# Row sums, 1 / rms and dilated shares through DRAM, and values overwritten by outputs, in a two-layer hybrid block

## The chip, the cores and the metric

One NeuronCore of a Trainium2 chip runs the whole program. The metric is the device time of one execution in microseconds (us). TensorE (PE) multiplies; VectorE (DVE), ScalarE (ACT) and GpSimd (POOL) work on elements; SyncE (SP) issues DMAs. Each engine runs its instructions in program order, and an instruction that waits holds up all those behind it on its engine.

## The reference

512 tokens of width 1024, two layers. Each layer adds a mixer, a cross attention to a memory of 256 tokens, and a gated feed-forward part; each reads an RMS norm of x.

```python
def hybrid_mixer(h, ...):                    # h = rms_norm(x)
    r_q, r_k, r_v, r_g, g_q, g_k, g_v, g_a, g_b, g_z, d_q, d_k, d_v, gates = split(h @ w_in)
    q, k = rotate(r_q), rotate(r_k)                       # retention: 4 heads
    o = retention_chunked(q, k, r_v, log_gamma)           # chunks with a carried state
    o_ret = rms_norm(o, ret_norm_g) * silu(r_g)
    c_q, c_k, c_v = split(silu(causal_depthwise_conv([g_q, g_k, g_v])))
    g = -exp(a_log) * softplus(g_a + dt_bias)             # log decay
    # per chunk: gc = cumsum(g); decay = exp(gc_i - gc_j)
    # A = I + strict_lower((beta k) k^T * decay); solve A u = beta v, ...
    o = gated_delta_chunked(l2_norm(c_q), l2_norm(c_k), c_v, g, sigmoid(g_b))
    o_gdn = rms_norm(o, gdn_norm_g) * silu(g_z)
    for window, dilation in ((128, 1), (512, 4), (2048, 16)):
        o_g, lse_g = dilated_window_attention(rope(d_q), rope(d_k), d_v, ...)
    wts = softmax(lse over the three groups)              # the dilated shares
    o_dil = sum(wts * o_g)
    gate = sigmoid(gates)
    return sum(gate[i] * (o_i @ w_br_i) for i in (ret, gdn, dil)) @ w_out

for l in range(2):
    x = x + hybrid_mixer(rms_norm(x, ..), ..)
    x = x + memory_cross_attention(rms_norm(x, ..), rms_norm(mem, ..), ..)
    x = x + conv_gated_mlp(rms_norm(x, ..), ..)
return rms_norm(x, final_norm_g)
```

## The kernel before

Every large product is made of three matmuls (`mm3`, L213 to L215): weights and activations are split into a rounded half (`wh`, `xgh`) and a rest (`wl`, `xgl`). SP fetches a slab of weights (`w`, two buffers, L187), ACT rounds it to `wh` (L202), DVE subtracts to get `wl` (L203), three buffers each.

A scheduler orders the instructions of every engine by what it thinks will be ready; `first()` and `soon()` raise priorities. The mixer's main line goes from product to product (`rva`, `rg`, `g`, `rqk`, `dqk`, `dv`, gates), and short generators in a list `side` are stepped between its products, each up to its next `yield`: decays, inverse, attention and scan of the gated delta part, retention, heads. `finish()` drains the list.

- `rms` (L305): sums of squares by token through TensorE (`_ss`, L312), 1 / rms on DVE (`rc`), then a row of it over all partitions: one 128x128 matmul for each block of 128 tokens (`_rp`, L317) and a copy on ACT (L320). The mixer (`nm`) also wants it by strided tokens: four more `_ss` matmuls.
- `gdn_decays` (L424): running sums of the log decay by one matmul (`gps`), then their rows over all partitions by sixteen matmuls (`gr`, L464), from which ACT makes |difference| and exp.
- `gdn_inverse` (L484): blocks of A go through DRAM (`Ad`, `Ag`, `Td`; all issued on the queue `DQ`, which is SP's); 31 steps on DVE invert the 32x32 blocks (`fs` L517, `Tg` L519); four 32- and 64-wide rounds on TensorE (`y` L539, `x` L549) join them. `gk` (L498) is the last product that A needs.
- `gdn_scan` and `retention` carry states over the four token blocks; outputs `og` and `oret` have their own regions; retention is put into `side` after `finish()`, the heads after that.
- `dilated` (L748): shares by softmax over the groups, widened on POOL (`dw`) and turned into rows by 32 matmuls in two layers of 16 (`dr`, L839).

Of the kernel before, what the change touches and what calls it, by code (L numbers as in the profile page):

```python
# [9 lines left out]
F32 = mybir.dt.float32  # L10
# [8 lines left out]
P = 128  # L19
# [5 lines left out]
H = 4  # L25
# [76 lines left out]
def tile_hybrid(ctx, tc, xT, memT, pos, wts, cst, kst, prm, rows, outT):  # L102
    nc = tc.nc
    V, S, G, PE = nc.vector, nc.scalar, nc.gpsimd, nc.tensor
    DQ = nc.sync
# [252 lines left out]
    def load_x(src, pieces=((0, 4), (4, 8))):  # L358
        xt = [region(("r3", "r8")[i], [4, T], f"x{i}") for i in range(2)]
# [64 lines left out]
    def gdn_decays(l, ab, rb, res):  # L424
# [28 lines left out]
        V.tensor_scalar(gp, gps, -1.0, None, ALU.mult)  # L453
# [29 lines left out]
    def gdn_inverse(l, kT, ssv, res):  # L483
# [98 lines left out]
    def gdn_scan(l, kT, qT, vb, res):  # L582

        U, attn, ceg, eg, egl, ekl = (res[n] for n in ("A", "attn", "ceg", "eg", "egl", "ekl"))
        o = region("r2", [NB, H, P], f"og{l}")
        ssq = small("ssg", 16)
        res.update(og=o, ssg=ssq)
        S0 = None
        for b in range(NB):
            us = slice(b * H, (b + 1) * H)  # L590
            if b < NB - 1:
                kp = pg(f"kp{b}", (H, P))
                transposes(kp, lambda h: kT[:, h, blk(b)])
                ks = tg(f"ks{b}", (H, P))
                V.tensor_tensor(ks, kp, over(ekl[:, us], P), ALU.mult)
# [30 lines left out]
            yield 1  # L626
            if b:
                qS = pg(f"qS{b}", (H, P))
                for h in range(H):
                    PE.matmul(qS[:, h, :], lhsT=qT[:, h, blk(b)], rhs=S0[:, h, :], start=True, stop=True)  # L630
                V.tensor_tensor(o[:, b], qS, over(eg[:, us], P), ALU.mult)
            op = pg(f"op{b}", (H, P))
            for h in range(H):
                PE.matmul(op[:, h, :], lhsT=attn[:, b * H + h, :], rhs=vn[:, h, :], start=True, stop=True)
            if b:
                V.tensor_tensor(o[:, b], o[:, b], op, ALU.add)
            else:
                S.activation(o[:, b], op, AF.Copy)
            sq = tg(f"osq{b}", (H, P))
            for h in range(H):  # L640
                i = b * H + h
                S.activation(sq[:, h, :], o[:, b, h, :], AF.Square, accum_out=ssq[:, i:i + 1])
            if b < NB - 1:
# [11 lines left out]
    def retention(l, rqk, rv, dec, res):  # L655

        o = region("r7", [NB, H, P], f"oret{l}")
        ssq = small("ssr", 16)
        res.update(oret=o, ssr=ssq)
        ks, states = [], []  # L660
        for j in range(2):
            ks.append(tg(f"rk{j}", (NB - 1, P)))
            states.append(tg(f"rst{j}", (NB - 1, P)))
# [3 lines left out]
            V.tensor_tensor(ks[j].rearrange("p b (e d) -> p (b e) d", e=2),  # L667
                            tpz.rearrange("p b (e d) -> p (b e) d", e=2),
                            over(dec[:, K_KD + 6 * j:K_KD + 6 * j + 6], 64), ALU.mult)
        for j in range(2):  # L670
# [3 lines left out]
            sps = [pool(f"rs{h}", (NB, P)) for (h, r), pool in zip(pair, (pa, pg))]  # L674
# [20 lines left out]
            yield 1  # L695
            yield 1
            ips = [pool(f"ri{h}", (NB - 1, P)) for (h, r), pool in zip(pair, (pa, pg))]

            def before(b, e):
                r = pair[e][1]  # L700
                return PE.matmul(ips[e][:, b - 1, :], lhsT=rqk[r, j, blk(b)], rhs=states[j][r][:, b - 1],
# [3 lines left out]
            ops = [pool(f"ro{h}", (NB, P)) for (h, r), pool in zip(pair, (pa, pg))]  # L705
# [3 lines left out]
            for (h, r), ip, op in zip(pair, ips, ops):  # L709
                S.activation(o[:, :, h, :], op, AF.Copy)  # L710
# [37 lines left out]
    def dilated(l, dq, dk, dv0, dv12, kc):  # L748
# [64 lines left out]
        for i, o in enumerate((oA, oB)):  # L813
# [593 lines left out]
```

## Time and profile before

| | |
|---|---|
| three runs | 2114.33, 2116.84, 2120.52 us (median 2116.84) |
| profiled execution | 2120.04 us, span 2118.2 us, mean granted clock 0.993 |
| PE busy | 2070.4 us of the span, 98% |
| DVE, ACT, POOL busy | 64%, 44%, 20% |
| chain that ended last | PE 86%, DVE 9%, DMA 2% |
| DMA | 95 GB/s on average |

The time of an engine is read against the span, and within a stretch against the stretch's length; what is missing there is idle time. A matmul's own duration overlaps the next one, so its cost in a packed row is the distance from start to start.

### The profile page before, as it was taken

What the parts mean: (1) busy time and instruction counts of PE and PEld (TensorE: products, weight loads), DVE (VectorE), ACT (ScalarE), POOL (GpSimd) and SP (SyncE); (2) the same over time, 40 slices, a digit from 0 to 9 for tenths busy, and PEclk for the clock granted to TensorE, in tenths of its full rate; (3) what the DMA queues carried; (4) which work ended last, traced back from release to release, by engine and by line L of the source; (5) the groups of instructions that cost most, each with busy time, mean ns of one, the idle gap of its engine ahead of it and who ended that gap; (6) DMA issues with size and microseconds to landing.
All of it is one profiled execution on the core that took longest, in us unless ns stands there. A gap on an engine that the chain in (4) does not pass through costs nothing.

```text
span 2118.2 us, 28765 instructions
## 1 busy us (share of the span) xinstructions
PE 2070.4 (98%) x10697; PEld 1736.2 (82%) x10697; DVE 1359.2 (64%) x2479; ACT 926.9 (44%) x1897; POOL 423.4 (20%) x427
## 2 busy tenths in 40 slices
PE   7999999999999999999999999999999999999997
PEld 6787878788888888888888879787788888888886
DVE  6788566446577875476456964854565787745754
ACT  4654333443355543244344533344344464423433
POOL 7832101012130211011132220100222221100112
PEclk9999999999999999999999999999999999999998
DMA  4333212233332233333323242122323323332332
GB/s 146 100 106 104 75 51 95 71 115 110 99 110 86 94 100 95 95 100 100 111 90 99 80 109 70 48 88 95 117 90 90 119 81 100 100 95 95 100 95 85
DMA packets 69756, 201.52 MB, mean 95 GB/s; under 512 B 18352, under 2 KB 21296, under 8 KB 69104
## 3 DMA queue, kind: packets, MB, share of 16 engines
q1 hardware_dynamic: 67120, 192.28, 29.5%
q0 software_dynamic: 2352, 7.37, 1.2%
q8 instruction: 84, 1.38, 0.3%
q14 instruction: 56, 0.46, 0.1%
q10 hardware_dynamic: 144, 0.04, 0.0%
HBM read 192.78 MB, written 6.88 MB: 94 GB/s over the span
## 4 chain that ended last, share of the span: by engine, by line
PE 86%; DVE 9%; DMA 2%; issue 1%; ACT 1%; SPq 0%; DVEq 0%; ACTq 0%
PE gate L215 4%; PE gate L213 4%; PE gate L214 4%; PE uu L214 3%; PE ua L214 3%; PE uu L215 3%; PE ua L215 3%; PE uu L213 3%; PE ua L213 3%; PE dn L214 3%; PE dn L213 3%; PE dn L215 3%; PE dqk L213 2%; PE dqk L215 2%; PE dqk L214 2%; PE y L215 2%
## 5 line engine op out<-in xcount | busy, mean ns | idle before, releaser
L202 ACT ACTIVATE wh<-w 128x512 fp32r<-128x512 f32 (+2 forms) x689 | 428.8, 624 | 849.1 <-PE dn L214 128.7
L203 DVE TENSOR_TENSOR wl<-w,wh 128x512 fp32r<-128x512 f32 (+2 forms) x689 | 509.7, 742 | 346.1 <-ACT wh L202 326.4
L213 PE MATMUL gate<-xgh,wh 128*128 128x512 f32 x384 | 151.2, 394 | 0.9 <-ACT wh L202 0.9
L215 PE MATMUL gate<-xgh,wl 128*128 128x512 f32 x384 | 151.6, 395 | 0.0
L214 PE MATMUL gate<-xgl,wh 128*128 128x512 f32 x384 | 150.9, 393 | 0.0
L213 PE MATMUL ua<-xgh,wh 128*128 128x512 f32 x320 | 124.5, 389 | 0.0
L214 PE MATMUL ua<-xgl,wh 128*128 128x512 f32 x320 | 124.5, 389 | 0.0
L215 PE MATMUL ua<-xgh,wl 128*128 128x512 f32 x320 | 124.5, 389 | 0.0
L213 PE MATMUL uu<-xgh,wh 128*128 128x512 f32 x320 | 124.5, 389 | 0.0
L214 PE MATMUL uu<-xgl,wh 128*128 128x512 f32 x320 | 124.5, 389 | 0.0
L215 PE MATMUL uu<-xgh,wl 128*128 128x512 f32 x320 | 124.5, 389 | 0.0
L213 PE MATMUL dn<-ah,wh 128*128 128x512 f32 x308 | 119.8, 389 | 0.0
L214 PE MATMUL dn<-al,wh 128*128 128x512 f32 x308 | 119.8, 389 | 0.0
L1146 POOL TENSOR_TENSOR fya<-fya,fyu 128x512 f32<-128x512 f32 x44 | 72.9, 1657 | 222.9 <-DVE fyu L1130 221.1
L215 PE MATMUL dn<-ah,wl 128*128 128x512 f32 x308 | 116.1, 389 | 0.0
L303 POOL TENSOR_TENSOR acc<-acc,sq 128x512 f32<-128x512 f32 x41 | 60.6, 1479 | 243.5 <-ACT sq L302 242.4
L868 POOL TENSOR_TENSOR mg<-mg,g 128x512 f32<-128x512 f32 x32 | 46.3, 1448 | 245.0 <-DVE g L866 244.9
L377 POOL TENSOR_TENSOR rot<-rot,tab 128x512 f32<-128x512 f32 x32 | 49.5, 1550 | 227.5 <-DVE rot L376 163.4
L213 PEld LDWEIGHTS gate<-xgh,wh 128*128 128x128 f32 x384 | 72.2, 188 | 15.8 <-ACT wh L202 1.2
L215 PEld LDWEIGHTS gate<-xgh,wl 128*128 128x128 f32 x384 | 72.1, 188 | 15.5 <-issue 0.7
L214 PEld LDWEIGHTS gate<-xgl,wh 128*128 128x128 f32 x384 | 72.1, 188 | 15.5 <-issue 1.0
L213 PE MATMUL dqk<-xgh,wh 128*128 128x512 f32 x192 | 76.2, 397 | 2.6 <-DVE rot L376 1.1
(496 smaller groups left out, 5189.5 us busy)
## 6 DMA issues: line engine op xcount, KB each, us to landing
w<-in_wts SPq DMA_DIRECT2D x331, 512.0 KB, 3.6
tab<-tabs_d POOLq DMA_DIRECT2D x4, 512.0 KB, 4.4
x<-in_xT SPq DMA_DIRECT2D x2, 1024.0 KB, 6.1
mem<-in_memT POOLq DMA_DIRECT2D x8, 256.0 KB, 3.3
x_d<-x SPq DMA_DIRECT2D x8, 256.0 KB, 3.1
x<-x_d SPq DMA_DIRECT2D x2, 1024.0 KB, 6.6
out<-x SPq DMA_DIRECT2D x8, 256.0 KB, 2.3
w<-in_wts SPq DMA_DIRECT2D x7, 256.0 KB, 2.5
```

The source lines that it names most:

```text
L202: S.activation(wh[:, :m], w[:, o:o + m], AF.Copy)
L203: V.tensor_tensor(wl[:, :m], w[:, o:o + m], wh[:, :m], ALU.subtract)
L213: PE.matmul(out, lhsT=lh, rhs=rh, start=start, stop=False)
L214: PE.matmul(out, lhsT=lh, rhs=rl, start=False, stop=False)
L215: PE.matmul(out, lhsT=ll, rhs=rh, start=False, stop=stop)
L303: eng.tensor_tensor(acc, acc, sq, ALU.add)
L377: G.tensor_tensor(t, t, tab[:, 1, :], ALU.mult)
L868: G.tensor_tensor(mt, mt, g, ALU.add)
L1146: G.tensor_tensor(ya, ya, yu, ALU.mult)
```

## The change

Rows that TensorE made of short columns now go through DRAM: a DMA writes the column in the row's order, a second one reads it back to all partitions. That holds for `rms` (`_rd`, also for the strided order), for the running sums (`gd`, read straight into `attn`'s place, where ACT then works in place) and for the dilated shares (`sh`, `dr`). `DQ` becomes POOL's queue. `vb` stands in the place of `vT`, `og` in that of `vb`, `oret` in that of `rv`; regions are dealt anew. Retention and its head move from after `finish()` to the stage of the first `dqk` products, with PSUM tiles of one pool (`pa`) and smaller steps; `finish()` comes after the second `dqk` group; the tables of layer 0 are issued at once, no longer in `side`; in the scan and in the last round of the inverse steps are joined. The scan writes its output right after each state. Several buffers change their number.

```diff
-    DQ = nc.sync
+    DQ = nc.gpsimd
...
-        n = 2 * nb if perm else nb
-        rc, v = small("rc", 8, 3), small("rv", 8)[:, :n]
-        sp = pg(name + "_ss", (n,))
-        for b in range(n):
-            tok = blk(b) if b < nb else slice(b - nb, None, NB)
-            PE.matmul(sp[:, b:b + 1], lhsT=acc[:, tok], rhs=one, start=True, stop=True)
+        rc, v = small("rc", 8, 3), small("rv", 4)[:, :nb]
+        sp = pg(name + "_ss", (nb,))
+        for b in range(nb):
+            PE.matmul(sp[:, b:b + 1], lhsT=acc[:, blk(b)], rhs=one, start=True, stop=True)
         V.tensor_scalar(v, sp, 1.0 / D, EPS, ALU.mult, ALU.add)
-        rsqrt(rc[:, :n], v)
-        rps = pg(name + "_rp", (nb * P,))
-        for b in range(nb):
-            PE.matmul(rps[:, blk(b)], lhsT=rc[:, b:b + 1].to_broadcast([P, P]), rhs=ident,
-                      start=True, stop=True)
+        rsqrt(rc[:, :nb], v)
+
+        rd = dp.tile([nb * P], F32, name=name + "_rd")
         rr = tmp("row", [T], name + "_row", 1) if row is None else row
-        S.activation(rr, rps, AF.Copy)
+        with soon():
+            G.dma_start(rd.rearrange("(b p) -> p b", p=P), rc[:, :nb])
+            G.dma_start(rr, rd.partition_broadcast(P))
+        if perm:
+            G.dma_start(rc[:, nb:2 * nb], rd.rearrange("(p n) -> p n", n=NB))
         return rc, rr
...
+        gs = small("gs", 16)
+        V.tensor_copy(gs, gps)
+        V.tensor_scalar(gp, gs, -1.0, None, ALU.mult)
         S.activation(eg, gp, AF.Exp)
         A = region("r7", [16, P], f"A{l}")
         attn = region("r5", [16, P], f"attn{l}")
         res.update(A=A, attn=attn)
+        gd = dp.tile([16, P], F32, name=f"gd{l}")
+        with soon():
+            G.dma_start(gd.rearrange("u p -> p u"), gs)
+            G.dma_start(attn, gd.partition_broadcast(P))
+        yield 1
+        yield 1
+        S.activation(egl, attn[:, :, P - 1], AF.Exp, scale=-1.0)
         for b in range(NB):
-            yield 1
             us = slice(b * H, (b + 1) * H)
-            gr = pg(f"gr{b}", (H, P))
-            for h in range(H):
-                i = b * H + h
-                PE.matmul(gr[:, h, :], lhsT=gpos[:, i:i + 1].to_broadcast([P, P]), rhs=tri,
-                          start=True, stop=True)
-            S.activation(egl[:, us], gr[:, :, P - 1], AF.Exp, scale=-1.0)
-            for h in range(H):
-                i = b * H + h
-                S.activation(attn[:, i, :], gr[:, h, :], AF.Abs, bias=gp[:, i:i + 1])
+            for i in range(b * H, (b + 1) * H):
+                S.activation(attn[:, i, :], attn[:, i, :], AF.Abs, bias=gp[:, i:i + 1])
             S.activation(attn[:, us, :], attn[:, us, :], AF.Exp, scale=-1.0)
-            S.activation(ekl[:, us], attn[:, us, P - 1], AF.Copy)
             G.tensor_tensor(A[:, us, :], attn[:, us, :], again(low, H), ALU.mult)
+            yield 1
+        S.activation(ekl, attn[:, :, P - 1], AF.Copy)
+        for b in range(NB):
+            us = slice(b * H, (b + 1) * H)
             G.tensor_tensor(attn[:, us, :], attn[:, us, :], again(tri, H), ALU.mult)
...
-        o = region("r2", [NB, H, P], f"og{l}")
+        o = vb
...
-        o = region("r7", [NB, H, P], f"oret{l}")
+        o = rv.rearrange("p b (h d) -> p b h d", h=H)
...
-            sps = [pool(f"rs{h}", (NB, P)) for (h, r), pool in zip(pair, (pa, pg))]
+            sps = [pa(f"rs{h}", (NB, P)) for h, r in pair]
-            kvs = [pool(f"rS{h}", (NB - 1, P)) for (h, r), pool in zip(pair, (pa, pg))]
+            sts = []
+            for (h, r), sp in zip(pair, sps):
+                sts.append(ta(f"st{h}", (NB, P)))
+                V.tensor_tensor(sts[-1], sp, again(dec[:, h * P:(h + 1) * P], NB), ALU.mult)
+            yield 1
+            kvs = [pa(f"rS{h}", (NB - 1, P)) for h, r in pair]
             for (h, r), kv in zip(pair, kvs):
...
+            sh = dp.tile([NB * H, P], F32, name=f"sh{l}{i}")
+            G.dma_start(sh.rearrange("u p -> p u"), a)
             for hp in range(2):
-                wide = ta(f"dw{i}{hp}", (NB, 2, 64))
-                G.tensor_copy(wide, a.rearrange("p (n h o) -> p n h o", h=H, o=1)[:, :, 2 * hp:2 * hp + 2, :]
-                              .to_broadcast([P, NB, 2, 64]))
-                rows = pa(f"dr{i}{hp}", (NB, P))
-                for n in range(NB):
-                    PE.matmul(rows[:, n, :], lhsT=wide[:, n].rearrange("p h d -> p (h d)"), rhs=ident,
-                              start=True, stop=True)
+                rows = ta(f"dr{i}{hp}", (NB, P))
+                for e in range(2):
+                    G.dma_start(rows[halves[e]], sh.rearrange("(n h) p -> h n p", h=H)[2 * hp + e].partition_broadcast(64))
                 V.tensor_tensor(o[:, hp], o[:, hp], rows, ALU.mult)
...
+        if l == 0:
+            for _ in tables():
+                pass
         side.append(gdn_decays(l, ab, rb, res))
-        if l == 0:
-            side.append(tables())
...
-        vb = region("r4", [NB, H, P], f"vb{l}")
+        vb = vT.rearrange("p h (b t) -> p h b t", b=NB)
...
+        gh, gl = region("r5", [H, T], f"gh{l}", F32R), region("r6", [H, T], f"gl{l}", F32R)
+        rh, rl = region("r7", [H, T], f"rh{l}", F32R), region("r8", [H, T], f"rl{l}", F32R)
+
+        def retained():
+            yield from retention(l, rqk, rv, dec, res)
+            yield 1
+            yield from head_out(res["oret"], res["ssr"], rgz, rc, None, rh, rl, pa, "r")
+
+        side.append(retained())
         tab = load_tab(1, rr)
-        dqk = [region("r10", [4, T], f"dqk{l}0")]
+        dqk = [region(t, [4, T], f"dqk{l}{i}") for i, t in enumerate(("r10", "r4"))]
...
+        keys_and_queries(1)
         finish()
-        side.append(retention(l, rqk, rv, dec, res))
-        dqk.append(region("r1", [4, T], f"dqk{l}1"))
-        keys_and_queries(1)
-        gh, gl = region("r5", [H, T], f"gh{l}", F32R), region("r6", [H, T], f"gl{l}", F32R)
-        rh, rl = region("r3", [H, T], f"rh{l}", F32R), region("r8", [H, T], f"rl{l}", F32R)
-        dqk.append(region("r4", [4, T], f"dqk{l}2"))
-
-        def heads():
-            yield 1
-            yield from head_out(res["og"], res["ssg"], zgz, rc, rqs, gh, gl, pg, "g")
-            yield from head_out(res["oret"], res["ssr"], rgz, rc, None, rh, rl, pa, "r")
-
-        side.append(heads())
+        side.append(head_out(res["og"].rearrange("p h b d -> p b h d"), res["ssg"], zgz, rc, rqs, gh, gl, pg, "g"))
+        dqk.append(region("r1", [4, T], f"dqk{l}2"))
         keys_and_queries(2)
...
-        mg = [region(t, [4, T], f"mg{l}{i}") for i, t in enumerate(("r9", "r7"))]
+        mg = [region(t, [4, T], f"mg{l}{i}") for i, t in enumerate(("r9", "r3"))]
```

What this does to the order of instructions, at three places of layer 0. On SP before, around the DMAs behind the recursion (`Td` takes its result to DRAM, `T` and `A` are read from there; `w` are weights):

```order
L187 DMA w_28_2072<-in_wts 128x1024 [waits DMAHW7_49,DVE_49]
L522 DMA Td_1514<-Tg_1124 64x1024 [waits DVE_49]
L523 DMA Td_1514<-Ag_1123 64x1024 [waits DVE_49]
L532 DMA T_1517<-Td_1514 32x16x32 [waits DMAHW2_49]
L532 DMA T_1517<-Td_1514 32x16x32 x2
L529 DMA A_396<-Td_1514 32x16x32 [waits DMAHW3_49]
L529 DMA A_396<-Td_1514 32x16x32 [waits DMAHW0_49]
L529 DMA A_396<-Td_1514 32x16x32 [waits DMAHW1_49]
L529 DMA A_396<-Td_1514 32x16x32
L187 DMA w_29_2134<-in_wts 128x1024 [waits DVE_49]
```

On POOL after, the same DMAs (`tab` is a rotary table, `rot` a half of a rotation):

```order
L377 TENSOR_TENSOR rot<-rot,tab_1889 128x512 [waits DVE_49,Pool_49]
L387 DMA tab_2121<-tabs_d 128x1024 [waits DMASW2_49,DMASW3_49,DMASW1_49,Pool_49]
L527 DMA Td_1486<-Tg_1096 64x1024 [waits DVE_49]
L528 DMA Td_1486<-Ag_1095 64x1024 [waits DVE_49]
L537 DMA T_1489<-Td_1486 32x16x32 [waits DMASW4_49]
L537 DMA T_1489<-Td_1486 32x16x32
L537 DMA T_1489<-Td_1486 32x16x32 [waits DMASW0_49]
L534 DMA A_456<-Td_1486 32x16x32 [waits DMASW5_49]
L534 DMA A_456<-Td_1486 32x16x32
L534 DMA A_456<-Td_1486 32x16x32 [waits DMASW3_49]
L534 DMA A_456<-Td_1486 32x16x32
L377 TENSOR_TENSOR rot<-rot,tab_2121 128x512 [waits DVE_49] x3
```

The seven DMAs have left the weights' queue; on POOL they stand between the rotations of `rqk` and those of `dqk`.

On PE before, where the products `y` wait for `A`:

```order
L214 MATMUL rqk_2015<-xgl,wh_27_512_2022 128x512
L539 MATMUL y_1583<-A_396 32x32
L215 MATMUL rqk_2015<-xgh,wl_27_512_2023 128x512
L213 MATMUL rqk_2015<-xgh,wh_27_512_2022 128x512
L214 MATMUL rqk_2015<-xgl,wh_27_512_2022 128x512
L539 MATMUL y_1583<-A_396 32x32 x31
L215 MATMUL rqk_2015<-xgh,wl_27_512_2023 128x512
```

And after:

```order
L215 MATMUL dqk_2420<-xgh,wl_32_0_2424 128x512
L713 MATMUL ro_2300<-rv_160,st_2218 128x128 x4
L713 MATMUL ro_2301<-rv_160,st_2220 128x128 x2
L544 MATMUL y_1555<-A_456 32x32 x22
L720 MATMUL ri_2362<-rst_2158,rqk_1894 128x128
L544 MATMUL y_1555<-A_456 32x32 x9
L713 MATMUL ro_2301<-rv_160,st_2220 128x128 x2
L213 MATMUL dqk_2420<-xgh,wh_32_0_2423 128x512
L214 MATMUL dqk_2420<-xgl,wh_32_0_2423 128x512
```

Most of the `y` products have moved from the third unit of `rqk` into the fourth unit of the first `dqk` group (one of them stands in its third unit), and the retention's `ro` and `ri`, which came behind the whole scan before, stand around them.

On ACT before, around the first table load behind the running sums:

```order
L202 ACTIVATE wh_7_512_605<-w_7_599 128x512 [waits PE_49]
L471 ACTIVATE ekl<-attn_397 128x4 [waits Activation_49]
L469 ACTIVATE attn_397<-gr_490,gp 128x128
L352 ACT_TABLE_LOAD
L352 ACTIVATE sn_377<-ang_374 128x512 [waits Pool_49]
L401 ACT_TABLE_LOAD
L401 ACTIVATE gz<-rg_311,half 128x512 [waits PE_49]
L401 ACTIVATE gz<-rg_312,half 128x512 [waits PE_49]
L470 ACTIVATE attn_397<-attn_397 128x512 [waits Activation_49]
L401 ACTIVATE gz<-rg_313,half 128x512 [waits PE_49]
```

And after:

```order
L352 ACT_TABLE_LOAD
L352 ACTIVATE sn_309<-ang_306 128x512 [waits Pool_49]
L202 ACTIVATE wh_10_0_767<-w_10_765 128x512 [waits DMAHW2_49,PE_49,Activation_49]
L467 ACT_TABLE_LOAD
L467 ACTIVATE egl<-attn_457 128x16 [waits DMASW7_49]
L353 ACTIVATE ang_306<-ang_306 128x512 [waits Activation_49]
L412 ACTIVATE y_699<-cin_696,par 128x512 [waits DVE_49]
L413 ACTIVATE z_700<-cin_696,par 128x512
L471 ACTIVATE attn_457<-attn_457,gp 128x128 [waits Activation_49]
L471 ACTIVATE attn_457<-attn_457,gp 128x128 x9
L354 ACT_TABLE_LOAD
L354 ACTIVATE ang_306<-ang_306,c 128x512 [waits Activation_49]
```

Before, `attn` was made block by block as `gr` came from PE; now all of it waits for one DMA (the wait at `egl`), and two roundings of weights (`wh_10_512`, `wh_11_0`) stand behind it.

## Rows read from the trace of the kernel before

**Rows 1.** The first and fourth part of the page
```profile
PE 2070.4 (98%) x10697; PEld 1736.2 (82%) x10697; DVE 1359.2 (64%) x2479; ACT 926.9 (44%) x1897; POOL 423.4 (20%) x427
PE 86%; DVE 9%; DMA 2%; issue 1%; ACT 1%; SPq 0%; DVEq 0%; ACTq 0%
```

**Rows 2.** Stretches of the span: start:end, length, busy of each engine (instructions), clock, DMA
```profile
50.00:70.00 20.00, 17.31 (x86) 14.49 (x85) 8.58 (x11) 18.93 (x40) 17.22 (x16) 1.00 0.24 79
130.00:187.00 57.00, 55.93 (x274) 45.93 (x273) 55.83 (x119) 31.10 (x75) 13.25 (x17) 1.00 0.27 88
280.00:350.00 70.00, 64.60 (x359) 56.91 (x358) 56.92 (x139) 26.32 (x76) 11.10 (x9) 1.00 0.23 71
1310.00:1400.00 90.00, 85.77 (x464) 74.27 (x463) 67.12 (x161) 32.97 (x93) 10.52 (x8) 1.00 0.22 68
```

**Rows 3.** TensorE's groups by shape: records, busy, mean ns, idle before
```profile
L464 PE MATMUL gr<-c,gpos 128*128 128x128 f32 x64 | 8.6, 277 | 0.0
L839 PE MATMUL dr<-c,dw 128*128 128x128 f32 x64 | 8.4, 275 | 0.0
```

**Rows 4.** The chain that ended last, of several stretches: start, us, piece
```profile
41.33 0.91 PE rg L213 x4
...
619.57 0.79 PE nx_ss L312 x8
...
630.89 0.89 PE nx_rp L317 x8
...
1070.86 2.82 PE nm_ss L312 x16
```

**Rows 5.** The timeline of TensorE at four places: start, us, instruction
```profile
107.69 0.83 PE L498 MATMUL gk<-kT 128*128 128x128 f32 x6
...
193.19 0.22 PE L539 MATMUL y<-A 32*32 32x32 f32 x2 [1.02 <-DMA A<-Td]
...
1153.94 0.94 PE L498 MATMUL gk<-kT 128*128 128x128 f32 x7
...
1230.17 0.22 PE L539 MATMUL y<-A 32*32 32x32 f32 x2 [1.52 <-DMA A<-Td]
```

**Rows 6.** VectorE's groups by shape (first: 123.5 to 187 us; others: whole span)
```profile
L203 DVE TENSOR_TENSOR wl<-w,wh 128x512 fp32r<-128x512 f32 x20 | 15.3, 767 | 0.3 <-ACT wh L202 0.3
...
L375 DVE TENSOR_TENSOR rqk<-rqk,tab 128x512 f32<-128x512 f32 x8 | 5.5, 683 | 6.8 <-PE rqk L215 6.8
L376 DVE STREAM_SHUFFLE rot<-rqk 128x512 f32<-128x512 f32 x8 | 5.8, 726 | 0.0
```

**Rows 7.** The chain that ended last, 184 to 196 us
```profile
185.90 1.05 DVE Ag L520
186.96 3.11 DMA Td<-Ag
...
194.35 1.19 PE y L539 x62
```

**Rows 8.** The lines that issue DMAs from GpSimd: ns min/median/max, first and last start
```profile
L387 POOL DMA_DIRECT2D tab<-tabs_d x4: 577/586/597, 76.5 to 1251.0; - x4
...
L809 POOL DMA_DIRECT2D sd<-stA x2: 804/805/806, 405.4 to 1447.2; - x2
```

**Rows 9.** DMA issues: out<-in, count, KB each, median us from issue to landing
```profile
tab<-tabs_d POOLq DMA_DIRECT2D x4, 512.0 KB, 4.4
...
A<-Td SPq DMA_DIRECT2D x8, 64.0 KB, 2.9
...
sd<-stA POOLq DMA_DIRECT2D x2, 16.0 KB, 2.5
```

**Rows 10.** ScalarE's groups by shape, 40 to 75 us
```profile
L469 ACT ACTIVATE attn<-gr,gp 128x128 f32<-128x128 f32 x16 | 4.7, 380 | 0.0
...
L352 ACT ACT_TABLE_LOAD x1 | 1.3, 1283 | 0.0
```

**Rows 11.** Waits of TensorE: us in total, times, longest us
```profile
PE rva L213 <- ACT wh L202: 8.4, 1, 8.4
```

More of the change, by code (lines that the diff above doesn't have):

```diff
@@ L358, in load_x @@
     def load_x(src, pieces=((0, 4), (4, 8))):
-        xt = [region(("r3", "r8")[i], [4, T], f"x{i}") for i in range(2)]
+        xt = [region(("r7", "r8")[i], [4, T], f"x{i}") for i in range(2)]
         with first():
@@ L554, in gdn_inverse @@
         S.activation(Tm[32:64, :, 0:32], x32[32:64], AF.Copy, scale=-1.0)
-        for g in range(2):
-            yield 1
-            us = slice(8 * g, 8 * g + 8)
+        yield 1
+        halves = [slice(8 * g, 8 * g + 8) for g in range(2)]
+        yts = []
+        for g, us in enumerate(halves):
             y64 = pg(f"y64{g}", (8, 64))
@@ L584, in gdn_scan, with out @@
         U, attn, ceg, eg, egl, ekl = (res[n] for n in ("A", "attn", "ceg", "eg", "egl", "ekl"))
-        o = region("r2", [NB, H, P], f"og{l}")
+        o = vb
         ssq = small("ssg", 16)
         res.update(og=o, ssg=ssq)
-        S0 = None
+        S0, vn = None, None
+        def out(b, S0, vn):
+            us = slice(b * H, (b + 1) * H)
+            if b:
+                qS = pg(f"qS{b}", (H, P))
+                for h in range(H):
+                    PE.matmul(qS[:, h, :], lhsT=qT[:, h, blk(b)], rhs=S0[:, h, :], start=True, stop=True)
+                V.tensor_tensor(o[:, :, b], qS, over(eg[:, us], P), ALU.mult)
+            op = pg(f"op{b}", (H, P))
+            for h in range(H):
+                PE.matmul(op[:, h, :], lhsT=attn[:, b * H + h, :], rhs=vn[:, h, :], start=True, stop=True)
+            if b:
+                V.tensor_tensor(o[:, :, b], o[:, :, b], op, ALU.add)
+            else:
+                S.activation(o[:, :, b], op, AF.Copy)
+            sq = tg(f"osq{b}", (H, P))
+            for h in range(H):
+                i = b * H + h
+                S.activation(sq[:, h, :], o[:, h, b, :], AF.Square, accum_out=ssq[:, i:i + 1])
         for b in range(NB):
             us = slice(b * H, (b + 1) * H)
[L591 to L595, printed above, removed]
             if b == 0:
-                r = vb[:, 0]
+                r = vb[:, :, 0]
             else:
@@ L604, in gdn_scan @@
                     i = b * H + h
-                    V.scalar_tensor_tensor(r[:, h, :], kS[:, h, :], ceg[:, i:i + 1], vb[:, b, h, :],
+                    V.scalar_tensor_tensor(r[:, h, :], kS[:, h, :], ceg[:, i:i + 1], vb[:, h, b, :],
                                            ALU.mult, ALU.add)
+            if b < NB - 1:
+                kp = pg(f"kp{b}", (H, P))
+                transposes(kp, lambda h: kT[:, h, blk(b)])
+                ks = tg(f"ks{b}", (H, P))
+                V.tensor_tensor(ks, kp, over(ekl[:, us], P), ALU.mult)
             yield 1
@@ L625, in gdn_scan @@
                                                ALU.mult, ALU.add)
[L626 to L643, printed above, removed]
+                out(b, S0, vn)
                 S0 = S1
                 yield 1
+            else:
+                out(b, S0, vn)
     def together(calls):
@@ L695, in retention @@
             yield 1
[L696 to L701, printed above, removed]
-                                 start=True, stop=True)
-            together([lambda a=(b, e): before(*a) for b in range(1, NB) for e in range(2)])
-            ops = [pool(f"ro{h}", (NB, P)) for (h, r), pool in zip(pair, (pa, pg))]
+            ops = [pa(f"ro{h}", (NB, P)) for h, r in pair]
             for (h, r), st, op in zip(pair, sts, ops):
@@ L708, in retention, with before @@
                     PE.matmul(op[:, b, :], lhsT=st[:, b], rhs=rv[:, b, h * P:(h + 1) * P], start=True, stop=True)
-            for (h, r), ip, op in zip(pair, ips, ops):
                 S.activation(o[:, :, h, :], op, AF.Copy)
+            yield 1
+            ips = [pa(f"ri{h}", (NB - 1, P)) for h, r in pair]
+            def before(b, e):
+                r = pair[e][1]
+                return PE.matmul(ips[e][:, b - 1, :], lhsT=rqk[r, j, blk(b)], rhs=states[r][:, b - 1],
+                                 start=True, stop=True)
+            together([lambda a=(b, e): before(*a) for b in range(1, NB) for e in range(2)])
+            for (h, r), ip in zip(pair, ips):
                 for b in range(1, NB):
@@ L944, in values @@
             transposes(vp, lambda b: vT[:, h, blk(b)])
-            V.tensor_tensor(vb[:, :, h, :], vp, over(res["bk"][:, h::H], P), ALU.mult)
+            V.tensor_tensor(vb[:, h], vp, over(res["bk"][:, h::H], P), ALU.mult)
             done.append(h)
@@ L1222, in tile_hybrid @@
         rc, rr = rms(acc, NB, f"nx{l}")
-        oh, ol = region("r0", [H, T], f"xoh{l}", F32R), region("r7", [H, T], f"xol{l}", F32R)
+        oh, ol = region("r0", [H, T], f"xoh{l}", F32R), region("r3", [H, T], f"xol{l}", F32R)
         cross(l, (mgh, mgl), mrc, mrow, rr, oh, ol)
```

33 lines of the change are left out of this document (13 added, 20 removed).

## Prediction

> **What bounds the kernel now.** I read the page first: TensorE is busy 2070.4 of 2118.2 us, and the chain that ended last is 86% PE and 9% DVE [rows 1]. So there are two ways to win: take work from PE, or take away PE's idle time, which is 47.8 us in all. Then I asked for PE's idle time by stretches. It lies almost wholly in the two mixers. The reader should look at two kinds of stretch. From 130 to 187 us DVE is busy 55.8 of 57 us: there the chain runs through DVE, and PE, busy 55.9, only just keeps up. From 280 to 350 and from 1310 to 1400 us, where retention and the heads run, PE lacks 5.4 and 4.2 us [rows 2]. The rest of the kernel (cross attention, feed-forward) is packed, so PE work that goes there is a gain in full.
>
> A packed 128x512 matmul costs 0.91 / 4 = 0.228 us from start to start, a plain 128x128 one 0.89 / 4 = 0.22 (eight records are four matmuls), a transpose, one record, 0.11 [rows 4]. I take 0.114 for a 128x256 one, an estimate from half the columns.
>
> **PE work removed.** `gr` and `dr` are 64 records each [rows 3]: at 0.89 us for eight [rows 4], 7.1 us each. The four kinds of `_rp` are by the program 56 records: 6.2 us. The strided sums: `nm_ss` takes 2.82 us for sixteen records, `nx_ss`, which has no strided ones, 0.79 for eight [rows 4], so 2.0 us in each layer, 4.1. Together 24.5 us. The row copies on ACT and the `dw` copies on POOL go too; neither engine sets the end there, so they count nothing. Nothing is added on PE.
>
> **The recursion.** Before, the last `gk` ends at 108.5 us and the first `y` starts at 193.2, so 84.7 us pass; in layer 1 it is 1154.9 and 1230.2, so 75.3 [rows 5]. By the order, PE does there 254 (layer 1: 244) matmuls of 512 columns, 96 of 256, 32 (28) transposes and 16 products `ap`: 254 x 0.228 + 96 x 0.114 + 32 x 0.11 + 16 x 0.22 = 75.9 us, in layer 1 73.2. It loses 8.8 and 2.1 us, because `y` waits for the chain `Ag` copy, `Td`, `A` [rows 7] behind a saturated DVE.
>
> After, the `y` products stand later: 358 matmuls of 512, 29 of 256, 35 transposes and 30 products come first, 95.4 us; in layer 1 304, 96, 32 and 16, 87.3 us. But more DVE work stands before the recursion's end too. In layer 0: two more `wl` at 0.77, three more rotations of `rqk` at 0.68 + 0.73 + 0.68 [rows 6], the third step counted like L375, and some 1 us net of other evictions: 1.5 + 6.3 + 1.1 = 8.9 us. In layer 1 the same count gives 7.7.
>
> The DMAs behind it: before, the copy ends at 186.95 and the bulk of `y` starts at 194.35, 7.4 us [rows 7]. After, POOL issues one `Td` half behind the copy (0.6), waits for its landing (3.1), issues four `A` (4 x 0.6 = 2.4), and the last lands 2.9 us later: 9.0 us [rows 7 to 9]. I take 2 us more than before.
>
> So the chain needs 84.7 + 8.9 + 2 = 95.6 us for 95.4 us of PE work, and 75.3 + 7.7 + 2 = 85.0 for 87.3. The loss goes from 8.8 to about 1 and from 2.1 to about 1 (I leave 1 us each for waits on the way): a gain of 9. If the chain were late by 5 us more in each layer, the gain would be nothing. Behind the seven DMA issues on POOL stand the rotations of `dqk`: POOL is held for some 8.5 us, DVE's third rotation step waits for it, and `wl` behind that. DVE has about 10 us of its own work ahead of that step, so I cost it at nothing; without that cover it is up to 8.5 us per layer.
>
> **Retention and heads.** They bunch up behind the scan: DVE is busy 56.9 of 70 us, and PE lacks 5.4 and 4.2 us [rows 2]. Half of that work now runs beside the first `dqk` products. I let half of the idle time go: 4.8 us. The bounds are 0 and 9.6.
>
> **Rows through DRAM.** A write and a read take about 0.8 + 2.5 and 0.6 + 4.4 us [rows 8, 9], 8.3 us from the column to the row; before, PE and ACT needed about 2. For `nm`, `nk` and `nf` whole groups of products lie between and hide it. For `nx` the first eviction of the cross attention's queries waits; PE can go on into other PSUM tiles for most of it: 1 us lost per layer, 2 in all (bounds 0 and 10). No row shows a write of 2048 single values (`gd`, `sh`); the nearest are 0.59 us for a table of 128 long rows and 0.805 for 512 short pieces [rows 8]. By that slope it is 0.8 + 1536 x 0.00057 = 1.7 us, an estimate; the lower bound is 0.8. `sh` is read one branch later, hidden.
>
> **The decays in layer 0.** From 50 to 70 us ACT is busy 18.9 and POOL 17.2 of 20 us, and PE lacks 2.7 [rows 2]. ACT's sixteen |differences| at 0.38 and its table loads at 1.28 [rows 10] stay. After, all of them wait for one load of `attn`, which POOL issues behind three multiplications; I put its landing at about 62 us. Two roundings of weights stand behind it on ACT. I count 4.2 us of idle time for 2.7: 1.5 lost (bounds: 3 gained, 8 lost).
>
> **The sum.** -24.5 - 9 - 4.8 + 2 + 1.5 = -34.8 us on the profiled execution's 2120.04 (its span and about 2 us around it): 2085. That execution was 3.2 us above the median of 2116.84 and within the three runs; on the median it would be 2082. I say 2083.
>
> **A rule against the change.** The POOL queue is where the rows and a rule part. The table loads issued by POOL take 0.577 to 0.597 us each [rows 8], and they land 4.4 us later for 512 KB [rows 9]; nothing there looks starved. The Trainium skill, "SBUF — State Buffer", section "SBUF: two separate sides", says that GpSimd writes the descriptors of the DMAs it issues, and cannot while VectorE copies in a mode that holds their shared port; its example goes from about 620 to about 3100 ns. By that figure the 28 DMAs of the inverse would cost 28 x 2.5 = 69 us more; it is a reason for the first rival below, which is worked out without it.
>
> **Rivals.**
> - *POOL's queue becomes the bound; slower.* 28 DMAs of the inverse (14 in each layer: `Ad`, `Ag`, `Td`, `T`, `A`) now go one behind the other on POOL, on the one chain that has no slack. If each costs c instead of 0.6 us there, the end moves by 28 x (c - 0.6), and the gain of 34.8 is gone from c = 1.85 on. With c = 2.9, a whole landing [rows 9], it is +64 - 35 = +29: 2149, on the median 2146. For it: POOL waits in order, and rotations stand behind. Against it: the rows of the table loads.
> - *Only the removed work counts.* The waits move and stay as large: -24.5 + 3.5 = -21: 2099, on the median 2096. For it: an in-order machine with a saturated DVE finds a new place to wait. Against: PE has 14 to 20 us more work before `y`.
> - *The mixers' idle time goes altogether.* 47.8 us less the start, 8.4 [rows 11], and some 7 that I leave for the last norm and the output, an estimate, is 32; with 24.5 it is -57: 2063, on the median 2060. For it: each stage gets slack at once. Against: DVE stays saturated from 130 us on.
> - *The change does not do what it says:* the order shows the removed matmuls gone, so I give this none.
>
> **Chances.** Forecast 0.46, only the work 0.20, all idle time 0.13, POOL's queue 0.21. Runs of this kernel differ by 0.3% (2114.33 to 2120.52), so 0.3%, 6.4 us, is what can be told from no change. Forecast, work alone and idle time are all faster by more; within POOL's queue c near 1.85 gives no change. Faster 0.73, same 0.07, slower 0.20. The range goes from 2056, a little past the case without idle time, to 2126, where POOL's queue costs 2.1 us for each DMA; the forecast's own range is 2070 to 2095.
>
> **What would show it.** Right: no `gr`, `dr`, `_rp` on PE; `y` without a wait of more than 2 us; `Td` and `A` issued from POOL at about 0.6 us each; PE's idle time some 37 us in all instead of 47.8; cross attention and feed-forward of the old length but for the rows. Wrong: `y`, or `wl` behind a rotation, waits for POOL or its DMAs for over 5 us per layer; ACT sits at `egl` for over 5 us while PE waits for `wh`; or PE's first product behind each norm waits for a row.

## The result, and the profile after

The changed kernel takes 2195.09 us (median of four runs, 2193.12 to 2198.93) where the kernel before takes 2117.10: 1.037 of it, 95% interval 1.0349 to 1.0391. It is 78 us slower; 35 us faster was forecast.

The page of the changed kernel, engine line [rows 1]:

```profile
PE 2072.2 (94%) x10497; PEld 1731.0 (79%) x10497; DVE 1379.8 (63%) x2481; ACT 919.1 (42%) x1875; POOL 469.0 (21%) x489
```

The span of 2197.2 us is 79.0 longer. PE's idle time is 2197.2 - 2072.2 = 125.0 us where it was 47.8; that is 77.2 of the 79.0. Its busy time has not fallen, though the matmuls are gone. The reason shows in the waits of PE after (us in total, times, longest):

```profile
PE g L213 <- ACT wh L202: 15.1, 2, 10.6
PE ua L213 <- DVE cfa L1138: 11.9, 2, 6.4
PE nx_ss L310 <- POOL acc L303: 11.7, 2, 6.0
PE xq L215 <- DVE wl L203: 9.1, 2, 5.2
PE gate L215 <- DVE wl L203: 9.1, 2, 5.5
PE rva L213 <- ACT wh L202: 8.4, 2, 8.1
...
PE gate L213 <- ACT wh L202: 7.1, 3, 6.0
...
PE y L544 <- DMA A<-Td: 3.9, 2, 2.6
```

The wait of `rva` was there before [rows 11], `y` waited then too [rows 5], and `gate` waited 0.9 us for `wh`. The others are new, and are for ACT's `wh`, DVE's `wl` and `cfa`, POOL's `acc`: engines that are held up by something else. The DMA issues after (columns as in [rows 9]) name it:

```profile
tab<-tabs_d POOLq DMA_DIRECT2D x4, 512.0 KB, 4.1
...
nm_row<-nm_rd POOLq DMA_DIRECT2D x2, 256.0 KB, 4.5
...
A<-Td POOLq DMA_DIRECT2D x8, 64.0 KB, 4.3
...
sh<-k POOLq DMA_DIRECT2D x4, 8.0 KB, 11.3
...
nm_rd<-rc POOLq DMA_DIRECT2D x2, 2.0 KB, 9.3
...
gd<-gs POOLq DMA_DIRECT2D x2, 8.0 KB, 11.9
sd<-stA POOLq DMA_DIRECT2D x2, 16.0 KB, 2.5
...
nk_rd<-rc POOLq DMA_DIRECT2D x2, 1.0 KB, 9.7
nx_rd<-rc POOLq DMA_DIRECT2D x2, 2.0 KB, 9.0
nf_rd<-rc POOLq DMA_DIRECT2D x2, 2.0 KB, 9.4
```

All the writes of a column to DRAM (`_rd`, `gd`, `sh`), of 1 to 8 KB, take 9.0 to 11.9 us to land. The write of 16 KB that was there before, `sd`, still takes 2.5, and the table load 4.1. The norms' rows are read back in 4.2 to 4.5 us, as forecast; `attn`, 1 MB, takes 7.2. Two stretches of the changed kernel, and the first one's place in the kernel before (columns as in [rows 2]):

```profile
480.00:520.00 40.00, 27.66 (x103) 21.56 (x103) 18.16 (x28) 9.21 (x17) 10.88 (x12) 0.83 0.44 92
280.00:350.00 70.00, 70.00 (x373) 62.02 (x372) 53.24 (x115) 21.68 (x54) 12.72 (x9) 1.00 0.25 82
```

```profile
475.00:520.00 45.00, 45.00 (x228) 37.25 (x227) 29.62 (x57) 18.38 (x37) 13.84 (x14) 1.00 0.35 107
```

In the second, where PE lacked 5.4 us before, it lacks nothing. In the first, in the dilated stage, it lacks 12 of 40 us, where it lacked nothing before, and the granted clock is 0.83: a part of the stretch ran at 1.2 instead of 2.4 GHz, after PE's idle time. Right behind a wait of 6.00 us the gate products stand 0.43 us apart from start to start; from 493 us on it is 0.23 again. Over the whole span the granted clock is 0.971, before 0.993. That is why PE's busy time has not fallen.

What holds it, on POOL and then on DVE (start, us, instruction, idle before and its releaser):

```profile
476.95 1.18 POOL L848 DMA_DIRECT2D sh<-k  x1
...
489.19 2.48 POOL L852 DMA_DIRECT2D dr<-sh  x4 [9.97 <-DMA sh<-k]
```

```profile
488.38 0.18 DVE L838 TENSOR_TENSOR k<-k,stB 128x16 f32<-128x16 f32 x1 [10.62 <-DMA sh<-k]
```

POOL issues `sh` at 476.95 and stands 9.97 us until it has landed, because the reads `dr` are next in its order. DVE wants to write over the buffer that the DMA still reads, and stands 10.62 us. ACT, which takes DVE's result, stands as long; behind that, on ACT, stand the roundings of the weights (`wh`), and PE waits 6.0 us for them at its next gate product.

At the decays it is the row's own reader. In layer 1 ACT stands at `egl`, which reads `attn`, and PE waits for the rounded weights behind it; this is the longest single wait of the list:

```profile
1158.06 0.23 ACT L467 ACTIVATE egl<-attn 128x16 f32<-128x16 f32 x1 [12.87 <-DMA attn<-gd]
```

```profile
1161.76 0.80 PE L213 MATMUL g<-xgh,wh 128*128 128x512 f32 x1 [10.57 <-ACT wh L202]
```

At the norms it is POOL's order, and again a reader. POOL after, and PE behind it:

```profile
631.25 0.72 POOL L317 DMA_DIRECT2D nk_rd<-rc  x1 [1.58 <-DVE rc L289]
641.24 0.58 POOL L318 DMA_DIRECT2D macc<-nk_rd  x1 [9.27 <-DMA nk_rd<-rc]
641.85 1.27 POOL L303 TENSOR_TENSOR acc<-acc,sq 128x512 f32<-128x512 f32 x1
653.66 0.77 POOL L317 DMA_DIRECT2D nx_rd<-rc  x1 [10.55 <-DVE rc L289]
662.38 0.55 POOL L318 DMA_DIRECT2D nx_row<-nx_rd  x1 [7.96 <-DMA nx_rd<-rc]
```

```profile
643.17 1.87 PE L310 MATMUL nx_ss<-c,acc 128*128 128x1 f32 x8 [5.69 <-POOL acc L303]
```

The write of the memory's 1 / rms lands 9.3 us late for its own read; behind that read stands `acc`, the sum of squares of another norm, and PE waits 5.69 us for it. Then `nx_rd` takes its own 8 us. The row of the feed-forward's norm is late for its reader on DVE, `cfa`, for which PE waits 6.4 us at `ua`:

```profile
758.35 0.69 DVE L1138 TENSOR_TENSOR cfa<-up,nf_row 128x512 f32<-128x512 f32 x1 [9.85 <-DMA nf_row<-nf_rd]
```

There is one more way, on another queue. A weight fetch of SP that is issued while a column's write is on its way is late too. The fetch next behind `nf_rd` in the changed kernel (745 to 747 us), then in `row_write`, an experiment below that writes the same values in longer pieces (718 to 722 us):

```profile
w<-in_wts SPq DMA_DIRECT2D x1, 512.0 KB, 11.8
```

```profile
w<-in_wts SPq DMA_DIRECT2D x1, 512.0 KB, 4.5
```

The median of all fetches is 3.5 us in both. For the fetch behind `gd` ACT's `wh` waits:

```profile
64.95 0.63 ACT L202 ACTIVATE wh<-w 128x512 fp32r<-128x512 f32 x1 [7.04 <-DMA w<-in_wts]
```

How much of the 78 us comes by each of these ways is not shown.

### The profile page after: what moved, and what is told of

The parts are those of the page before. It is cut to its first block, busy times and chain, and to the rows that moved or that the text cites. A ratio compares the mean times of both kernels' runs of the same rounds, so it can differ in the third digit from the quotient of the medians.

```text
span 2197.2 us, 28429 instructions
## 1 busy us (share of the span) xinstructions
PE 2072.2 (94%) x10497; PEld 1731.0 (79%) x10497; DVE 1379.8 (63%) x2481; ACT 919.1 (42%) x1875; POOL 469.0 (21%) x489
## 5 line engine op out<-in xcount | busy, mean ns | idle before, releaser
L203 DVE TENSOR_TENSOR wl<-w,wh 128x512 fp32r<-128x512 f32 (+2 forms) x689 | 515.7, 751 | 344.3 <-ACT wh L202 318.8
L213 PE MATMUL ua<-xgh,wh 128*128 128x512 f32 x320 | 126.4, 395 | 11.9 <-DVE cfa L1138 11.9
L213 PE MATMUL g<-xgh,wh 128*128 128x512 f32 x192 | 77.4, 403 | 16.5 <-ACT wh L202 15.1
```

Source lines behind the costliest of these rows:

```text
L203: V.tensor_tensor(wl[:, :m], w[:, o:o + m], wh[:, :m], ALU.subtract)
L213: PE.matmul(out, lhsT=lh, rhs=rh, start=start, stop=False)
```

## The experiments

Theory A: the writes in pieces of 4 bytes land late, and the rows' readers, the order of POOL, and buffers that the DMA still reads pass the delay to all engines. Rival B: GpSimd's queue itself is the cost, above all for the inverse's DMAs. Rival C: the earlier retention and the shared places are. Rival D: GpSimd makes its descriptors slowly. Kernels of one group ran on one chip, each group on another; the first result's chip is not on record. The kernel before took 2120.25, 2120.29 and 2120.46 us in the three groups.

**Group 1: take one kind of row back to TensorE.** `rms_pe`:

```diff
-            G.dma_start(rd.rearrange("(b p) -> p b", p=P), rc[:, :nb])
-            G.dma_start(rr, rd.partition_broadcast(P))
+            PE.matmul(rps[:, blk(b)], lhsT=rc[:, b:b + 1].to_broadcast([P, P]), rhs=ident, ...)
+        S.activation(rr, rps, AF.Copy)
```

> The changed kernel with only the rows of 1 / rms made by TensorE again (_rp matmuls, strided _ss, copy on ACT). Theory A (the writes of single 4-byte values to DRAM land after 9 to 12 us instead of the 2.5 us that I had put in, and GpSimd, which waits for them in order, passes the delay on): from the end of wo to the first ua, 128 us in each layer now, falls back to 108, so about 40 us less in all: 2155 us. Rival B (what hurts is GpSimd's queue as such, with the DMAs of the inverse): only the DMAs' own time goes, at most 10 us: 2185 us. Rival C (the earlier retention and the shared places cost the time): no change beyond the 10 us of TensorE work that come back: 2195 to 2205 us.

2153.31 us, 1.0153 (1.0132 to 1.0174). `dec_pe`:

```diff
-            G.dma_start(gd.rearrange("u p -> p u"), gs)
-            G.dma_start(attn, gd.partition_broadcast(P))
+                PE.matmul(gr[:, h, :], lhsT=gpos[:, i:i + 1].to_broadcast([P, P]), rhs=tri, ...)
```

> The changed kernel with only the running sums' rows made by TensorE again (gr matmuls instead of gd and the load of attn). Theory A: the 12 us of gd and 7 us of attn go from the chain to gk; layer 0 reaches its last gk at 128 us instead of 108 before, layer 1 loses about as much, so 20 to 30 us less with 7 us of TensorE work back: 2172 us. Rival B: 2190 us. Rival C: about 2200 us.

2196.40 us, 1.0352 (1.0329 to 1.0375). `dil_pe`:

```diff
-            G.dma_start(sh.rearrange("u p -> p u"), a)
-                    G.dma_start(rows[halves[e]], sh...partition_broadcast(64))
+                G.tensor_copy(wide, a...to_broadcast([P, NB, 2, 64]))
+                    PE.matmul(rows[:, n, :], lhsT=wide[:, n]..., rhs=ident, ...)
```

> The changed kernel with only the dilated shares widened by GpSimd and made into rows by TensorE again (dw, dr instead of sh). Theory A: the waits at the first gates (6.0, 0.9 and 5.5 us in layer 0) go, the stage from the first gate to wo falls from 229 and 226 us to 220 and 221: 13 us less, 2182 us. Rivals B and C: 2195 to 2202 us.

2187.73 us, 1.0318 (1.0291 to 1.0345). `all_pe`, the three edits together:

> The changed kernel with all three kinds of rows made by TensorE again; the early retention, the shared places, and the inverse's DMAs on GpSimd's queue stay. Theory A: all that was lost comes back, 40 + 23 + 13 = 76 us: 2119 us, and less if the early retention saves the idle time that I forecast (2105). Rival B: the inverse's DMAs on GpSimd's queue still cost, 2140 us or more. Rival C: 2150 us or more.

2110.71 us, 0.9952 (0.9934 to 0.9971): all is back, and some more. That fells C. Against the first result, 2195, the single gains (42, none, 7) do not add up to 84; `dec_pe` looks like a miss. But its writes of the norms landed after 10.5 to 10.9 us, those of the first profile after 9.0 to 9.7. Within this one chip, each kernel's distance from `all_pe` is the cost of the rows it still sends through DRAM: norms + decays 77.0 us, norms + shares 85.7, decays + shares 42.6. Solved, if the three costs simply add up, the norms cost 60.1, the decays 16.9, the shares 25.6, together 102.6 us. So the changed kernel should take 2213 us on such a chip.

**Group 2.** `after_again` is the changed kernel with no edit:

> The changed kernel itself once more, on the same chip as the three beside it, because the writes of dec_pe landed after 10.7 us where those of the first profile took 9.0 to 9.7. Theory A: the landing of the small writes differs from chip to chip, and the ratio to the kernel before moves with it: between 1.035 and 1.045 here, 2195 to 2210 us.

2214.95 us, 1.0446 (1.0417 to 1.0474); its writes landed after 10.0 to 12.6 us. So the three costs add up to within 2 us, taken over two chips, and this kernel differs by 20 us from the first result, the kernel before by 3. Whether the chip makes that difference is not shown. `row_write`, all three kinds of rows through DRAM, but turned by TensorE first:

```diff
+        PE.matmul(tq[:nb], lhsT=rc[:, :nb], rhs=ident, start=True, stop=True)
+        S.activation(rt[:nb], tq[:nb], AF.Copy)
-            G.dma_start(rd.rearrange("(b p) -> p b", p=P), rc[:, :nb])
+            G.dma_start(rd.rearrange("(b p) -> b p", p=P), rt[:nb])
```

and the same with `gs` to `gd` and the shares to `sh`.

> The changed kernel, but each column is first turned into rows by one TensorE matmul and a small copy on ScalarE, so that all writes to DRAM are 2, 4 or 16 pieces of 512 bytes instead of 256, 512 or 2048 pieces of 4. Theory A (the number of 4-byte pieces makes the write slow): the writes land after 2 to 3 us, each chain is 6 to 9 us shorter, and two thirds of the loss go: about 2140 us. Rival B (any trip through DRAM by GpSimd's queue costs this much): the writes stay at 9 us or so, 2190 us or more.

2114.43 us, 0.997 (0.9956 to 0.9984; ten runs). 100 us are gone by this edit alone, more than expected. Its DMA issues, its engine line, and the dilated stage:

```profile
sh<-sw POOLq DMA_DIRECT2D x4, 8.0 KB, 3.3
...
nm_rd<-nm_rt POOLq DMA_DIRECT2D x2, 2.0 KB, 1.9
...
gd<-gt POOLq DMA_DIRECT2D x2, 8.0 KB, 2.5
...
nk_rd<-nk_rt POOLq DMA_DIRECT2D x2, 1.0 KB, 1.6
nx_rd<-nx_rt POOLq DMA_DIRECT2D x2, 2.0 KB, 1.6
```

```profile
PE 2053.2 (97%) x10525; PEld 1713.9 (81%) x10525; DVE 1382.7 (65%) x2481; ACT 924.0 (44%) x1889; POOL 467.7 (22%) x489
```

```profile
475.00:520.00 45.00, 45.00 (x200) 36.82 (x199) 28.64 (x45) 18.73 (x35) 12.51 (x15) 1.00 0.42 124
```

The same bytes in pieces of 512 land after 1.6 to 3.3 us. PE has no idle time in the stage, and its busy time is 2053.2 us, 17 below before: here the removed matmuls show. They show in PE's work alone: `row_write` has 14 us less of it than `all_pe` (2067.3), and takes as long (0.997 and 0.9952 of the kernel before). `hw_write`:

```diff
-            G.dma_start(rd.rearrange("(b p) -> p b", p=P), rc[:, :nb])
+            S.dma_start(rd.rearrange("(b p) -> p b", p=P), rc[:, :nb])
```

> The changed kernel, but the writes of 1 / rms (512 or 256 pieces of 4 bytes, as before) are issued by ScalarE instead of GpSimd. Theory A: the pieces are the cost, the write still lands after 8 us or more, and the time stays within 10 us of the changed kernel. Rival D (GpSimd makes the descriptors of its DMAs slowly): the write lands after 2.5 to 4 us, and most of what rms_pe won comes back: about 2165 us.

2217.55 us, 1.0463 (1.0432 to 1.0495), as slow as `after_again`. Its writes:

```profile
nm_rd<-rc ACTq DMA_DIRECT2D x2, 2.0 KB, 11.2
...
nx_rd<-rc ACTq DMA_DIRECT2D x2, 2.0 KB, 10.4
```

ScalarE's queue makes them no faster: D falls for the norms' writes, the ones that were moved. `all_pe_sp` is `all_pe` with one line back:

```diff
-    DQ = nc.gpsimd
+    DQ = nc.sync
```

> The kernel all_pe (all rows by TensorE, early retention) with the inverse's DMAs back on SyncE's queue. Theory A: their queue matters little; the landings fall by 1.3 us at three places of the chain to y, so 0 to 8 us less than all_pe, 2103 to 2111 us. Rival B (GpSimd's queue is the cost): 15 us or more less, below 2097 us. If the weights queue behind them again, 5 us more: 2116 us.

2103.72 us, 0.9919 (0.989 to 0.9947): 7 us less than `all_pe`, though on another chip, and the intervals of the two ratios meet.

**Group 3.** `rms_dec_pe`, the edits of `rms_pe` and `dec_pe`:

> The changed kernel with 1 / rms and the running sums by TensorE again, the dilated shares still through DRAM in 4-byte pieces. rms_pe alone gained 42 us, dec_pe alone next to nothing, dil_pe 7, and all three together 84. If the slow writes of the mixer's norm and of the running sums lie side by side, so that either alone still holds the stage, then this one has all but the dilated part: 2118 to 2125 us. If instead the missing 36 us belong to the dilated stage together with another, it stays near 2150 us.

2141.15 us, 1.010 (1.0079 to 1.0122), a miss: the shares alone cost 30 us beside `all_pe`, not 13. I had read 13 from the length of one stage against before, and the slow clock and the work saved were in it. The 30 us are between two chips; solved within one, it was 25.6. In its dilated stage, from 475 to 520 us, PE is busy 31.45 us at a granted clock of 0.85, and DVE waits 12.26 us for `sh` to land.

`nk_pe`, only the memory's norm back on TensorE:

```diff
-        mrc, mrow = rms(macc, 2, f"nk{l}", row=mm[:, 1])
+        mrc, mrow = rms_pe(macc, 2, f"nk{l}", row=mm[:, 1])
```

> The changed kernel with only the memory's 1 / rms (nk, read late by anyone but GpSimd's queue) made by TensorE. Theory A with GpSimd's order: its slow write holds no reader but what stands behind it on GpSimd, the sums acc for the next norm; so the wait of nx_ss for acc (11.7 us in both layers) goes and 12 to 16 us are gained: about 1.038 of the kernel before on this chip, 2200 us. If order does not matter and only readers of a row wait: no change, 2215 us.

2200.72 us, 1.0374 (1.0355 to 1.0393): 14 us below `after_again`, which ran on another chip. No wait is left for `nx_ss`, which was 13.0 us in `after_again`; `ua` (14.5) and `xq` (12.4) wait as there (14.1 and 12.8). That part of the order's cost is shown by the wait; its size across chips is less sure. The edit also takes away the wait of the row's own reader (`kf` on DVE, 9.76 us in the changed kernel), so the order is not shown to be all of it. `before_dq`, the kernel before with one line changed:

```diff
-    DQ = nc.sync
+    DQ = nc.gpsimd
```

> The kernel before with only the inverse's DMAs moved to GpSimd's queue. Theory A: their landing is about 1.3 us longer at four places of a chain that has no slack, in both layers: 10 us, less what the weights' queue gains: 2124 to 2131 us. Rival B: 28 DMAs at 1.2 us more or worse, over 2150 us.

2133.87 us, 1.0061 (1.0039 to 1.0083): 13 us slower, 3 more than the upper end that was expected. B is real, but small. Its POOL in layer 0:

```profile
210.90 0.59 POOL L387 DMA_DIRECT2D tab<-tabs_d  x1
211.49 0.55 POOL L523 DMA_DIRECT2D Td<-Ag  x1
...
220.75 2.57 POOL L529 DMA_DIRECT2D A<-Td  x4 [5.08 <-DMA Td<-Ag]
```

The `A` reads are issued 9.3 us behind `Td`, before it was 3.1, and a table load has come ahead of `Td` in the queue; DVE waits 6.47 us for that one. `mix`, `all_pe_sp` with the norm of the mixer and the running sums of layer 1 as in `row_write`:

> The kernel all_pe_sp, but in layer 1 alone the mixer's norm and the running sums go through DRAM as in row_write (turned by TensorE first, written in 512-byte pieces). In row_write layer 1 went from its first product to its last gk in 90 us, in all_pe_sp in 96, because GpSimd has no tables to make there; in layer 0 it was 120 against 104. If this holds outside row_write: 6 us less than all_pe_sp, 2097 us; if the difference came from elsewhere in row_write, 2104 us.

2100.19 us, 0.9903 (0.9886 to 0.9921). The fastest, but its interval overlaps that of `all_pe_sp`; whether it is faster stays open. Both beat the kernel before.

## Why the prediction was wrong

- **The failed step is "Rows through DRAM".** I took 0.8 + 2.5 us for a write from `sd` [rows 8, 9], 8.3 us from column to row, and 2 us of loss in all (bounds 0 and 10), with 1.5 more for the decays of layer 0. Measured: landing 9.0 to 9.7 us for the norms, 11.3 to 11.9 for `sh` and `gd`. `sd` goes in pieces of 32 bytes, these in pieces of 4. I scaled the issue time by the number of pieces (1.7 us; measured 1.17 to 1.23 on POOL) and did not bound the landing at all. In group 1 the three uses cost 60, 17 and 26 us, if they add up. The Trainium skill, "DMA: Bandwidth & Descriptors", section "Rules for kernel authors", says that a non-contiguous last dimension becomes one descriptor per element, and to make it contiguous; `row_write` bears the advice out with 100 us. The page gives no time for it.
- **The hiding failed too.** "Whole groups of products lie between" did not hold for the rows' readers: `cfa` waits 9.85 us for the row of `nf`, and `kf` 9.76 us for that of `nk`. Nor did it cover what stands behind the reads on POOL (`acc`, rotations, `mg`), or the buffer that DVE writes next; for `nk` and `sh` I named neither. For the decays I looked at layer 0 alone. In layer 1 came what I had named as a sign of being wrong: ACT stands at `egl` for 12.87 us while PE waits for `wh`. That a slow write also delays the weights on SP's queue I did not think of.
- **PE work removed (24.5 us): right as work, not as time.** PE's busy time falls by 17.2 us in `row_write`, which has put 14 small products back. In the changed kernel the slow clock hides it. And where the rows go through DRAM fast, other waits take the place of the work: `row_write` is no faster than `all_pe`, which does that work.
- **Retention and heads (4.8 us, bounds 0 and 9.6): right in kind, half the size.** In `all_pe_sp`, which has no PE work less, PE lacks nothing in the stages where it lacked 5.4 and 4.2 us [rows 2]:

```profile
280.00:350.00 70.00, 70.00 (x326) 60.60 (x325) 50.18 (x107) 24.48 (x57) 13.35 (x9) 1.00 0.30 91
1300.00:1390.00 90.00, 90.00 (x466) 78.56 (x466) 64.30 (x152) 35.41 (x93) 12.74 (x9) 1.00 0.26 79
```

  `all_pe_sp` is 17 us faster than before, and I forecast 14 from this and the recursion. That the two numbers are near is luck: the recursion gave nothing in it. From the last `gk` to the first `y` it takes 84.0 and 75.5 us (before 84.7 and 75.3), and `y` waits for `A` 3.9 us in all (before 2.9). What is shorter is the stage from the first gate to the last: 212.4 and 212.1 us, before 220.6 and 221.7. A part of the dilated products (`ds`, `dt`) now stands ahead of it, in the stretch where PE had idle time before.
- **The recursion (9 us of gain): there was none.** I put down 8.8 us of layer 0 to the wait of `y`, as what was left after a count of matmuls. The trace before has only 4.7 us of idle time of PE there (1.5 in layer 1), and 2.9 us of waits for `A` in both layers. With `y` behind more products, in `all_pe`, PE is idle for no less: 6.3 us (2.9 in layer 1). Layer 0 before, then in `all_pe`, from the last `gk` to `y`:

```profile
108.50:193.20 84.70, 79.97 (x416) 66.72 (x416) 75.47 (x160) 44.27 (x94) 25.37 (x28) 0.98 0.37 103
```

```profile
112.70:224.80 112.10, 105.80 (x542) 86.22 (x542) 94.74 (x187) 46.70 (x101) 41.31 (x46) 1.00 0.36 104
```

  The DMAs were undersized as well: I took 9.0 us from the copy's end to `y`. In the changed kernel DVE, POOL and PE show

```profile
220.73 1.05 DVE L525 COPY Ag<-Tg 64x1024 f32<-64x1024 f32 x1
```

```profile
222.07 0.55 POOL L528 DMA_DIRECT2D Td<-Ag  x1 [0.18 <-issue]
225.59 1.99 POOL L537 DMA_DIRECT2D T<-Td  x3 [2.97 <-DMA Td<-Tg]
227.58 2.57 POOL L534 DMA_DIRECT2D A<-Td  x4
```

```profile
232.59 0.21 PE L544 MATMUL y<-A 32*32 32x32 f32 x2 [2.57 <-DMA A<-Td]
```

  so 232.59 - 221.78 = 10.8 us in layer 0; the landings are 4.3 instead of 2.9 us, and three issues of `T`, 2 us, stand ahead of `A`, which I had not counted.
- **The rivals.** The one that ends slower had the right engine and the wrong price: 28 DMAs of the inverse at a whole landing each. They cost 13 us in `before_dq` and 7, between two chips, from `all_pe_sp` to `all_pe`; the writes cost 100. The rule that stood beside it (the Trainium skill, "SBUF — State Buffer", section "SBUF: two separate sides": GpSimd cannot write descriptors while VectorE copies in a mode that holds their shared port) is not what these runs show: ScalarE's writes were as slow, with 10.4 us for `nx_rd`, and GpSimd's own in pieces of 512 bytes took 1.6. And from 480 to 485 us of the changed kernel VectorE did nothing at all, while `sh`, issued at 476.95, had not landed; the DMA engines were busy for 0.71 of that time and moved 21 GB/s:

```profile
480.00:485.00 5.00, 3.38 (x15) 2.45 (x14) 0.00 (x0) 0.00 (x0) 0.00 (x0) 1.00 0.71 21
```

## What to carry to other kernels

Before a value goes through DRAM, look at the size of its contiguous pieces, not its bytes: if they are single elements, turn the column into rows on TensorE first. A wait on an in-order engine is paid by all that stands behind it, by whoever reuses a buffer that the DMA still reads, and here also by the loads on other queues; list all three before calling a transfer hidden. Where no row shows a transfer of that shape, the nearest row is no bound.

## What the runs showed of the hardware that I had not expected

The landing hardly depends on how many 4-byte pieces there are: 256 (`nk_rd`) took 9.7 us, 512 (`nx_rd`) 9.0, 2048 (`gd`) 11.9, while 512 pieces of 32 bytes (`sd`) took 2.5. Why single elements are slow was not tried further. The same kernel differed in it on two occasions: `nx_rd` took 9.0 us in the first profile and 10.0 in `after_again`, and the kernel 1.037 and 1.0446 of the kernel before. Such a write is not slow alone: in `after_again` fetches of 512 KB of weights beside the columns' writes took up to 12.9 us, in `row_write`, on the same chip, none took over 6.1 once the start was over. ACT's `wh` waits for fetches 77.5 and 50.3 us in these two (59.9 in `all_pe`); what of that reaches the end is not shown. Idle time of PE costs twice: between 480 and 520 us it lost 12 us idle, and the granted clock there was 0.83.
